# Projections with their operand differences made in place, the first branch's sum kept on chip, and blocks read from PSUM

## The chip, the cores and the metric

The kernel runs on one NeuronCore of a Trainium2 chip. The metric is the device time of one execution in microseconds. Three runs of the kernel before took 1317.86, 1319.45 and 1319.67 us; the median is 1319.45.

## The reference

One step of a hybrid encoder layer on 1024 prompt rows and 64 sample rows, D_MODEL 1024, float32. Cut to what matters here:

```
h = RMSNorm(x) * (1 + scale) + shift
z = h @ w_in                       # split into a, g_a, u, v_b, g_b, q, k, v_c, g_c, z_lr, g_m
y_a = pool_mixer(a) * silu(g_a)    # 512 columns
y_b = sgu_mixer(u, v_b) * silu(g_b)  # 512 columns
y_c = rmsnorm(gla_scan(q, k, v_c, decay)) * silu(g_c)   # 1024 columns
gm = sigmoid(g_m)                  # three parts of 1024
m = gm[0] * (y_a @ w_oa) + gm[1] * (y_b @ w_ob) + gm[2] * (y_c @ w_oc)
x = x + gate * RMSNorm_post(m @ w_out)
```

## The kernel before

Every large product is done in float32 accuracy with split operands: a "hi" part (rounded to fp32r by ScalarE, a CAST) and a "lo" part (the rest, a subtraction on VectorE or GpSimd). A step is then three matmuls, hi x hi, hi x lo and lo x hi, each once per 272-column half of a 544-column piece: six matmuls per 128 rows of depth. The 1088 tokens are two pieces p of 544 columns (512 prompt and 32 sample).

Most products are in Strassen-Winograd form. `s_unit` (line 578) makes 256 output channels from four blocks A(i, j) of a weight matrix and seven operands named in `PRODUCTS` (B11, T2, B21, T3, T1, T4, B22). `strassen_b` (line 433) makes these seven from four blocks of the input: B11, B21 and B22 as they are, and the differences T1 = b12 - b11, T2 = b22 - T1, T3 = b22 - b12, T4 = b21 - T2; each of the seven is split into hi and lo. It is called for the layer's input h (`dst is Hb`), for the first branch (`Ab`, from z_ya, two blocks j) and for the third (`Cb`, from z_yc, four blocks j). The second branch (`plain_units`, line 1443) is a plain product with operands split by `pairs_in`; its result is multiplied by its gate, added to the first branch's sum, which is loaded from `z_m` in DRAM, and stored there again.

In a unit, seven products of nkk steps go through three PSUM pairs: pA, pB and `third` (pC). B11 goes to pA, is copied by ScalarE into pB, on which T2 adds; T1 goes to pC; B21 adds onto pA, which then holds block (0, 0); T3 adds onto pB. The last two products, T4 and B22, are left over (`unfinished`) and done by `finish_unit` inside the next unit, between its B11 and the copy into pB, or at the end of a stage. T4 gives block (1, 0) in pB; the blocks (0, 1) and (1, 1) are sums that VectorE makes in the staging tiles `u` and `c22`. Every block is first copied to a staging tile by ScalarE and handed to `post(i, p, t)`: for a silu gate (`post_gc`, `post_ga`, `post_gb`) tanh on ScalarE and (th + 1) * t on VectorE, for a sigmoid gate (`post_gm`) tanh, for a branch (`post_m`) (th + 1) * t with th loaded from `z_gm`.

With `feed`, as in the first units of a projection, the first three products are interleaved step by step: each of B11, T2, T1 for block j before the next j.

Order of the work: the q, k, v, gate and mixer units of `w_in` (34 units) with the attention heads woven in, the last twelve of them gate units g_m; then `blocks_in(z_ya)` and the first branch (w_oa, four units, nkk = 2) with `pairs_in(z_yb)` woven in; the second (w_ob, 16 pieces) with `blocks_in(z_yc)` for j = 0 to 2 woven in; the third (w_oc, four units, nkk = 4), whose first unit feeds j = 3; then the output product with w_out. From the first unit on, a planner sets the order on each engine: it places instructions by priority in program order on a simulated timeline; weights are raised by `ahead()`. On the chip each engine works through its own queue in that order.

Tiles: operands lie in 56 places h (and five more, `NH` on), listed for reuse in `free` and `rest` in the order of `PRODUCTS`, since that is the order in which the last unit of the stage before lets them go; loaded blocks and gates go through a ring of 12 tiles x (`cur["blk"]`); results and differences through a ring of 9 staging tiles (`stage`, tag s). In the trace, `h` is an operand place, `T` a difference, `raw`, `sf`, `hi`, `lo` the weights' parts, `sps` pA and pB, and `t`, `c`, `u` staging tiles. All instructions stand under the line of a helper (L70, `InOrder`), so rows are told apart by tiles.

Of the kernel before, what the change touches and what calls it, by code (L numbers as in the profile page):

```python
# [24 lines left out]
PC = TH + SH  # L25
# [21 lines left out]
PLAIN = ("B11", "B21")  # L47
PRODUCTS = ("B11", "T2", "B21", "T3", "T1", "T4", "B22")
H_PLACES = (
# [29 lines left out]
def tile_hybrid_pool_sgu_gla_step(  # L79
# [353 lines left out]
    def strassen_b(dst, j, b1, b2, alloc):  # L433
        b11, b12 = b1
        b21, b22 = b2

        def put(name, src, he, le):
            hl = (alloc(name), alloc(name))
            split(src, hl, he, le)
            dst[name][j] = hl  # L440
            places[name] += alloc.held[-2:]

        t1, t2, t3, t4 = (stage("T", F32)[:, 0:PC] for _ in range(4))
        put("B11", b11, act, dve)
        dve.tensor_sub(t1, b12, b11)
        dve.tensor_sub(t2, b22, t1)
        put("T2", t2, act, dve)
        put("T1", t1, act, dve if dst is Hb and j == 3 else pool)
        with behind() if dst is Hb and j == 3 else ExitStack():
            put("B21", b21, act, dve)  # L450
            pool.tensor_sub(t3, b22, b12)
            put("T3", t3, act, dve)
            pool.tensor_sub(t4, b21, t2)
            put("T4", t4, act, dve)
            put("B22", b22, act, pool)
# [122 lines left out]
    def s_unit(src, c0, Bb, nkk, post, off=0, raw=None, feed=None):  # L578
# [64 lines left out]
        else:  # L643
# [8 lines left out]
            act.copy(view(c22), vC)  # L652
            yield nkk
        product(pA, A(0, 1), "B21", False)
        c11 = stage("c11", F32)
        act.copy(view(c11), vA)
        post(0, 0, c11)
        yield nkk
# [6 lines left out]
        def rest():  # L665
            product(pB, A(1, 1), "T4", False)
            c21 = stage("c21", F32)
            act.copy(view(c21), vB)
            post(1, 0, c21)
            yield nkk  # L670
# [208 lines left out]
    def silu2(t):  # L879
# [3 lines left out]
        dve.scalar_tensor_tensor(t, th, 1.0, t, op0=ALU.add, op1=ALU.mult)  # L883

    def post_gc(head):
        def post(i, p, t):
            silu2(t[:, 0:PC])
            store(z_gc[2 * head + i], p, t[:, 0:PC])

        return post  # L890

    def post_gm(b0):
        def post(i, p, t):
            act.activation(t[:, 0:PC], t[:, 0:PC], AF.Tanh, scale=0.5)
            store(z_gm[b0 + i], p, t[:, 0:PC])

        return post

# [71 lines left out]
    def post_ga(unit):  # L970
        def post(i, p, t):
            g = 2 * unit + i
            silu2(t[:, 0:PC])
            yp = st.pop(("yp", g, p))
            pool.tensor_mul(t[:, 0:PC], t[:, 0:PC], yp[:, 0:PC])
            store(z_ya[g], p, t[:, 0:PC])

        return post

# [96 lines left out]
    def post_gb(unit):  # L1076
        def post(i, p, t):
            g = 2 * unit + i
            t = t[:, 0:PC]
            silu2(t)  # L1080
            u = st.pop(("u", g, p))
            dve.scalar_tensor_tensor(t, t, 0.5, u[:, 0:PC], op0=ALU.mult, op1=ALU.mult)
            store(z_ub[g], p, t)

        return post

# [279 lines left out]
    def pair_in(z, p, alloc, raw_alloc):  # L1366
# [3 lines left out]
        turn[0] += 1  # L1370
        split(t, hl, act, pool if turn[0] % 3 == 0 else dve)
        return hl
# [10 lines left out]
    def w_unit(src, c0, nk, alloc=None):  # L1383

        out = []
        for k0 in range(0, nk, 4):
# [4 lines left out]
            for j in range(2):  # L1391
# [7 lines left out]
                with ahead():  # L1399
                    act.copy(hi, s)  # L1400
                    (pool if turn[0] % 2 == 0 else dve).tensor_sub(lo, s, hi.bitcast(F32))
                out += [(hi[:, i, :], lo[:, i, :]) for i in range(2)]
        return out

    def post_m(br, u):

        def fetch(i, p):
            j = 2 * u + i
            th = load(z_gm[br * 8 + j], p * PC, PC, "gm", blk)[:, 0:PC]
            return th, br and load(z_m[j], p * PC, PC, "m", blk)[:, 0:PC]  # L1410

        early = {}
        if br == 2 and u == 3:
# [4 lines left out]
        def post(i, p, t):  # L1418
            j, t = 2 * u + i, t[:, 0:PC]
            th, m = early.get((i, p)) or fetch(i, p)  # L1420
            dve.scalar_tensor_tensor(t, th, 1.0, t, op0=ALU.add, op1=ALU.mult)
            if br:
                (pool if br == 2 and (p or u < 3) else dve).tensor_add(t, t, m)
            store(z_m[j], p, t)
# [8 lines left out]

    Bp = {}

    def pairs_in(z, dst, places_):
# [6 lines left out]
    def plain_units(w, src):  # L1443

        n = 0
        for u in range(4):
            with ahead():
                wk = w_unit(w, u * UC, 4)
            for i in range(2):
                j = 2 * u + i  # L1450
                for p in range(2):
# [16 lines left out]
                    )  # L1468
                    m = load(z_m[j], p * PC, PC, "m", blk)[:, 0:PC]
                    pool.tensor_add(t, t, m)  # L1470
                    store(z_m[j], p, t)
# [306 lines left out]
    with first:  # L1778
# [106 lines left out]
        weave(last_units(), last_heads(), R3)  # L1885
        run(gate_steps, finish_unit())
        tick(LATER)
# [19 lines left out]
    def units(w, blocks, nkk, br, us=range(4)):  # L1907
        for u in us:
            yield from s_unit(
                w, u * UC, blocks, nkk, post_m(br, u), feed=None if u else fed  # L1910
            )

    cur["more"] = ctx.enter_context(tc.tile_pool(name="more", bufs=1))
    rest = [*free[28:56], *range(NH, NH + 5)]
    weave(
        chain(units(woa, Ab, 2, 0), finish_unit()),
        pairs_in(z_yb, Bp, rest[0:16]),
        0.2,
    )
    rest = [*rest[16:], *a_free]  # L1920
    weave(
        plain_units(wob, Bp),
        blocks_in(z_yc, Cb, ((j, rest[14 * j : 14 * j + 14]) for j in range(3))),
        0.08,
    )
    last = blocks_in(z_yc, Cb, ((3, rest[42:45] + free[28:39]),))
    idle = free[39:44]
    msum.append(slot(idle.pop())[:, 0:512].rearrange("p (k n) -> p k n", k=KB))
# [92 lines left out]
```

## Time and profile before

| | |
|---|---|
| median of three runs | 1319.45 us |
| the profiled execution's own time | 1318.15 us |
| its span, first to last instruction | 1316.4 us |
| mean granted TensorE clock | 0.973 |
| TensorE busy | 1217.9 us, 93% of the span |
| VectorE busy | 914.5 us, 69% |
| ScalarE busy | 626.2 us, 48% |
| GpSimd busy | 444.2 us, 34% |
| DMA | 195.38 MB, mean 148 GB/s |

The span of the trace begins at 0 us. The last gate unit's products end near 984 us, the first branch's near 1040, the second's near 1092, the third's near 1189, and the output product follows. A matmul in the trace overlaps its neighbours, so a stretch in which TensorE is busy all the time can still hold more or fewer matmuls; the count per microsecond is the better measure.

### The profile page before, as it was taken

The numbers are of one execution on the slowest core, as the hardware profiler recorded it, in microseconds if no ns is written. First come the engines' busy times: TensorE is split into PE (matmuls) and PEld (weight loads), VectorE is DVE, ScalarE is ACT, GpSimd is POOL, SyncE is SP. The second block draws the span as 40 slices with busy tenths as digits, with TensorE's granted clock in tenths as the row PEclk, the third lists the DMA queues.
The fourth block names the chain that finished last, engine by engine and source line by source line (L and its number), as shares of the span: only waits on it lengthen the run. The fifth ranks groups of instructions, "written<-read, shape, count | busy, mean of one in ns | idle before, by whom it ended". The sixth has DMA issues, their size and how long they took to land.

```text
span 1316.4 us, 23815 instructions
## 1 busy us (share of the span) xinstructions
PE 1217.9 (93%) x8962; PEld 1139.5 (87%) x8962; DVE 914.5 (69%) x1507; ACT 626.2 (48%) x1259; POOL 444.2 (34%) x356
## 2 busy tenths in 40 slices
PE   5779999999999999999999999999997998996895
PEld 3279999998999999999999999999896997994674
DVE  6976845557746679675476969665467798669758
ACT  7547734454553434544444464544364423343533
POOL 4640211122411315131145322212132486448524
PEclk9889999999999999999999999999999999998898
DMA  8612533252332213323146444445446898665055
GB/s 285 200 50 99 179 107 93 75 162 90 120 102 80 84 57 100 120 72 119 33 138 219 152 159 146 156 124 157 134 137 213 301 333 294 210 231 185 23 198 201
DMA packets 144609, 195.38 MB, mean 148 GB/s; under 512 B 18505, under 2 KB 82047, under 8 KB 144494
## 3 DMA queue, kind: packets, MB, share of 16 engines
q1 hardware_dynamic: 144494, 193.86, 45.3%
q8 instruction: 70, 1.15, 0.4%
q14 instruction: 45, 0.37, 0.1%
HBM read 133.59 MB, written 60.22 MB: 147 GB/s over the span
## 4 chain that ended last, share of the span: by engine, by line
PE 62%; DVE 13%; DMA 10%; issue 8%; POOL 3%; ACT 2%; SPq 1%; DVEq 0%; POOLq 0%; ACTq 0%
PE sps L70 37%; PE third L70 15%; PE aps L70 9%; DVE x L70 4%; DVE h L70 3%; DVE lo L70 1%; DMA x<-z_bc 1%; DMA raw<-in_w_in_dram 1%; DMA h<-z_m 1%; DMA x<-z_yc 1%; DMA h<-in_x_prompt_dram 1%; SPq L72 1%; DMA h<-in_ada_w_dram 1%; POOL T L70 1%; DMA x<-z_yb 1%
## 5 line engine op out<-in xcount | busy, mean ns | idle before, releaser
L70 PE MATMUL sps<-h,hi 128*128 128x272 f32 x3344 | 588.4, 295 | 14.9 <-DVE h L70 4.5
L70 PEld LDWEIGHTS sps<-h,hi 128*128 128x128 f32 x3344 | 482.6, 190 | 24.7 <-DVE h L70 4.9
L70 PE MATMUL sps<-h,lo 128*128 128x272 f32 x1672 | 353.5, 291 | 0.0
L70 PEld LDWEIGHTS sps<-h,lo 128*128 128x128 f32 x1672 | 265.8, 190 | 2.3 <-issue 1.7
L70 PE MATMUL third<-h,hi 128*128 128x272 f32 x1344 | 237.5, 294 | 6.8 <-ACT h L70 1.9
L70 PEld LDWEIGHTS third<-h,hi 128*128 128x128 f32 x1344 | 193.9, 189 | 11.7 <-issue 3.1
L70 DVE TENSOR_TENSOR lo<-sf,hi 128x512 fp32r<-128x512 f32 (+1 forms) x168 | 119.5, 712 | 92.7 <-ACT hi L70 87.3
L70 ACT CAST hi<-sf 128x512 fp32r<-128x512 f32 (+1 forms) x168 | 100.2, 598 | 157.7 <-PE sps L70 119.2
L70 POOL TENSOR_TENSOR sf<-raw 128x512 f32<-128x512 f32 (+1 forms) x38 | 49.5, 1301 | 303.7 <-DVE lo L70 238.4
L70 DVE TENSOR_TENSOR lo<-raw,hi 128x512 fp32r<-128x512 f32 (+1 forms) x130 | 99.2, 764 | 73.8 <-ACT hi L70 54.6
L70 ACT CAST hi<-raw 128x512 fp32r<-128x512 f32 (+1 forms) x134 | 80.1, 599 | 144.4 <-PE sps L70 97.2
L70 PE MATMUL third<-h,lo 128*128 128x272 f32 x672 | 142.4, 291 | 1.2 <-DVE lo L70 1.1
L70 POOL TENSOR_TENSOR x<-x,x 128x256 f32<-128x256 f32 (+2 forms) x71 | 74.9, 1065 | 123.3 <-ACT x L70 89.2
L70 PEld LDWEIGHTS third<-h,lo 128*128 128x128 f32 x672 | 106.8, 190 | 1.7 <-DVE lo L70 1.6
L70 POOL TENSOR_TENSOR sf<-raw,sf 128x512 f32<-128x512 f32 (+1 forms) x38 | 49.3, 1298 | 170.6 <-DVE lo L70 165.7
L70 ACT ACTIVATE x<-x 128x512 f32<-128x512 f32 (+2 forms) x104 | 57.5, 568 | 89.8 <-DVE x L70 80.2
L70 DVE TENSOR_TENSOR x<-x 128x256 f32<-128x256 f32 (+4 forms) x142 | 76.6, 571 | 27.8 <-DMA x<-z_bc 16.7
L70 DVE TENSOR_TENSOR x<-x,x 128x256 f32<-128x256 f32 (+4 forms) x100 | 64.2, 656 | 9.2 <-ACT x L70 8.8
L70 DVE TENSOR_TENSOR h<-h,h 128x544 fp32r<-128x544 f32 (+4 forms) x47 | 53.2, 1150 | 11.9 <-DMA h<-in_w_out_dram 6.9
L70 PE MATMUL aps<-x,x 128*128 128x256 f32 (+6 forms) x352 | 54.4, 290 | 2.3 <-ACT vt L70 1.8
L70 DVE TENSOR_TENSOR sf<-raw,raw 128x512 f32<-128x512 f32 (+1 forms) x42 | 33.0, 785 | 30.2 <-POOL sf L70 29.9
L70 POOL TENSOR_TENSOR sm<-sm,nhalf 128x1 f32<-128x1 f32 (+3 forms) x36 | 26.8, 748 | 75.4 <-DVE sm L70 75.4
(273 smaller groups left out, 1797.1 us busy)
## 6 DMA issues: line engine op xcount, KB each, us to landing
raw<-in_w_in_dram SPq DMA_DIRECT2D x68, 512.0 KB, 3.8
x<-z_gm SPq DMA_DIRECT2D x48, 272.0 KB, 3.3
z_gm<-c SPq DMA_DIRECT2D x36, 272.0 KB, 2.3
x<-z_m SPq DMA_DIRECT2D x32, 272.0 KB, 4.5
h<-z_m SPq DMA_DIRECT2D x28, 272.0 KB, 5.1
h<-in_x_prompt_dram SPq DMA_DIRECT2D x28, 256.0 KB, 5.4
z_m<-c SPq DMA_DIRECT2D x24, 272.0 KB, 2.4
h<-in_ada_w_dram SPq DMA_DIRECT2D x24, 256.0 KB, 4.5
```

The lines of the kernel that those rows point to most:

```text
L70: return f(*args, **kw)
L72: self._last = f(*args, **kw)
```

## The change

- `strassen_b` for the branches (not for Hb): one staging tile t2 in place of four; T1 is written over b11, T3 over b12, T4 over b21. The order is B11, T2, T1, B21, T3, T4, B22, and so is `PRODUCTS`. The low parts of T1 and B22 go from GpSimd to VectorE, as do the second branch's (a third of them) and half of w_ob's; T3's and T4's differences stay on GpSimd.
- `s_unit`: the blocks (0, 0) and (1, 0) go through `out`: where the post has a `direct` form, it works from PSUM, without the copy.
- The first branch's products by its gate are written to 16 places `m_first` on chip and not stored; the second branch adds them with VectorE, where it loaded `z_m` and added with GpSimd.
- The first branch's first unit has no `feed`; the last gate unit's T4 and B22 are left over into it.
- The places: operands of the second branch on the last places of the unit before and four more; the third branch's blocks 0 and 1 on those of the first branch, 2 on two further places and on `m_first`'s, 3 on the rest and on the second branch's. One place more in all.

```
@@ -45,7 +45,7 @@
 PLAIN = ("B11", "B21")
-PRODUCTS = ("B11", "T2", "B21", "T3", "T1", "T4", "B22")
+PRODUCTS = ("B11", "T2", "T1", "B21", "T3", "T4", "B22")
 H_PLACES = (
...
@@ -440,13 +440,28 @@
+        if dst is not Hb:
+            t2 = stage("T", F32)[:, 0:PC]
+            put("B11", b11, act, dve)
+            dve.tensor_sub(b11, b12, b11)
+            dve.tensor_sub(t2, b22, b11)
+            put("T2", t2, act, dve)
+            put("T1", b11, act, dve)
+            put("B21", b21, act, dve)
+            pool.tensor_sub(b12, b22, b12)
+            put("T3", b12, act, dve)
+            pool.tensor_sub(b21, b21, t2)
+            put("T4", b21, act, dve)
+            put("B22", b22, act, dve)
+            return
+
         t1, t2, t3, t4 = (stage("T", F32)[:, 0:PC] for _ in range(4))
...
         put("T2", t2, act, dve)
-        put("T1", t1, act, dve if dst is Hb and j == 3 else pool)
-        with behind() if dst is Hb and j == 3 else ExitStack():
+        put("T1", t1, act, dve if j == 3 else pool)
+        with behind() if j == 3 else ExitStack():
             put("B21", b21, act, dve)
...
@@ -651,10 +666,17 @@
             yield nkk
+        def out(i, ps):
+            direct = getattr(post, "direct", None)
+            if direct:
+                direct(i, 0, ps)
+            else:
+                t = stage("c", F32)
+                act.copy(view(t), ps)
+                post(i, 0, t)
+
         product(pA, A(0, 1), "B21", False)
-        c11 = stage("c11", F32)
-        act.copy(view(c11), vA)
-        post(0, 0, c11)
+        out(0, vA)
         yield nkk
...
@@ -664,9 +686,7 @@
             product(pB, A(1, 1), "T4", False)
-            c21 = stage("c21", F32)
-            act.copy(view(c21), vB)
-            post(1, 0, c21)
+            out(1, vB)
             yield nkk
...
@@ -882,18 +902,37 @@
+    def silu2_of(ps):
+
+        th, t = blk("th")[:, 0:PC], stage("t", F32)[:, 0:PC]
+        act.activation(halves(th), ps, AF.Tanh, scale=0.5)
+        dve.scalar_tensor_tensor(halves(t), halves(th), 1.0, ps, op0=ALU.add, op1=ALU.mult)
+        return t
+
+    def silu_post(done):
+
+        def post(i, p, t):
+            t = t[:, 0:PC]
+            silu2(t)
+            done(i, p, t)
+
+        post.direct = lambda i, p, ps: done(i, p, silu2_of(ps))
+        return post
+
     def post_gc(head):
-        def post(i, p, t):
-            silu2(t[:, 0:PC])
-            store(z_gc[2 * head + i], p, t[:, 0:PC])
-
-        return post
+        return silu_post(lambda i, p, t: store(z_gc[2 * head + i], p, t))
...
+        def direct(i, p, ps):
+            t = stage("t", F32)[:, 0:PC]
+            act.activation(halves(t), ps, AF.Tanh, scale=0.5)
+            store(z_gm[b0 + i], p, t)
+
+        post.direct = direct
         return post
...
@@ -968,14 +1007,13 @@
     def post_ga(unit):
-        def post(i, p, t):
+        def done(i, p, t):
             g = 2 * unit + i
-            silu2(t[:, 0:PC])
             yp = st.pop(("yp", g, p))
-            pool.tensor_mul(t[:, 0:PC], t[:, 0:PC], yp[:, 0:PC])
-            store(z_ya[g], p, t[:, 0:PC])
-
-        return post
+            pool.tensor_mul(t, t, yp[:, 0:PC])
+            store(z_ya[g], p, t)
+
+        return silu_post(done)
...
@@ -1074,15 +1112,13 @@
     def post_gb(unit):
-        def post(i, p, t):
+        def done(i, p, t):
             g = 2 * unit + i
-            t = t[:, 0:PC]
-            silu2(t)
             u = st.pop(("u", g, p))
...
-        return post
+        return silu_post(done)
...
@@ -1368,7 +1404,7 @@
         turn[0] += 1
-        split(t, hl, act, pool if turn[0] % 3 == 0 else dve)
+        split(t, hl, act, dve)
         return hl
...
@@ -1398,7 +1434,7 @@
                     act.copy(hi, s)
-                    (pool if turn[0] % 2 == 0 else dve).tensor_sub(lo, s, hi.bitcast(F32))
+                    dve.tensor_sub(lo, s, hi.bitcast(F32))
                 out += [(hi[:, i, :], lo[:, i, :]) for i in range(2)]
...
@@ -1408,6 +1444,13 @@
             return th, br and load(z_m[j], p * PC, PC, "m", blk)[:, 0:PC]
+
+        def place(i, p):
+
+            if br:
+                return stage("t", F32)[:, 0:PC]
+            t = m_first[2 * u + i, p] = slot(m_places[4 * u + len(m_first) % 4])
+            return t
...
@@ -1416,11 +1459,27 @@
         def post(i, p, t):
-            j, t = 2 * u + i, t[:, 0:PC]
             th, m = early.get((i, p)) or fetch(i, p)
-            dve.scalar_tensor_tensor(t, th, 1.0, t, op0=ALU.add, op1=ALU.mult)
-            if br:
-                (pool if br == 2 and (p or u < 3) else dve).tensor_add(t, t, m)
+            src = t[:, 0:PC]
+            t = src if br else place(i, p)
+            dve.scalar_tensor_tensor(t, th, 1.0, src, op0=ALU.add, op1=ALU.mult)
+            done(i, p, t, m)
+
+        def direct(i, p, ps):
+            th, m = early.get((i, p)) or fetch(i, p)
+            t = place(i, p)
+            dve.scalar_tensor_tensor(
+                halves(t), halves(th), 1.0, ps, op0=ALU.add, op1=ALU.mult
+            )
+            done(i, p, t, m)
+
+        post.direct = direct
+
+        def done(i, p, t, m):
+            j = 2 * u + i
+            if not br:
+                return
+            (pool if p or u < 3 else dve).tensor_add(t, t, m)
             store(z_m[j], p, t)
...
@@ -1432,6 +1491,7 @@
     Bp = {}
+    m_first, m_places = {}, []
...
@@ -1466,8 +1526,7 @@
                     )
-                    m = load(z_m[j], p * PC, PC, "m", blk)[:, 0:PC]
-                    pool.tensor_add(t, t, m)
+                    dve.tensor_add(t, t, m_first.pop((j, p)))
                     store(z_m[j], p, t)
...
@@ -1883,7 +1942,7 @@
         weave(last_units(), last_heads(), R3)
-        run(gate_steps, finish_unit())
+        run(gate_steps)
         tick(LATER)
...
@@ -1907,24 +1966,27 @@
             yield from s_unit(
-                w, u * UC, blocks, nkk, post_m(br, u), feed=None if u else fed
+                w, u * UC, blocks, nkk, post_m(br, u), feed=None if u or not br else fed
             )
...
     cur["more"] = ctx.enter_context(tc.tile_pool(name="more", bufs=1))
-    rest = [*free[28:56], *range(NH, NH + 5)]
+    m_places.extend(free[28:44])
+    b_places = [*free[44:56], *range(NH, NH + 4)]
     weave(
         chain(units(woa, Ab, 2, 0), finish_unit()),
-        pairs_in(z_yb, Bp, rest[0:16]),
+        pairs_in(z_yb, Bp, b_places),
         0.2,
     )
-    rest = [*rest[16:], *a_free]
+    c_places = [*a_free, NH + 4, NH + 5, *m_places]
+    for p in range(2):
+        c_places += [i for n, i in enumerate(b_places) if n // 2 % 2 == p]
     weave(
         plain_units(wob, Bp),
-        blocks_in(z_yc, Cb, ((j, rest[14 * j : 14 * j + 14]) for j in range(3))),
+        blocks_in(z_yc, Cb, ((j, c_places[14 * j : 14 * j + 14]) for j in range(3))),
         0.08,
     )
-    last = blocks_in(z_yc, Cb, ((3, rest[42:45] + free[28:39]),))
-    idle = free[39:44]
+    last = blocks_in(z_yc, Cb, ((3, c_places[42:56]),))
+    idle = c_places[56:]
     msum.append(slot(idle.pop())[:, 0:512].rearrange("p (k n) -> p k n", k=KB))
...
```

## Rows read from the trace of the kernel before

**Rows 1.** The page's busy times: busy us (share of the span) xinstructions.

```profile
PE 1217.9 (93%) x8962; PEld 1139.5 (87%) x8962; DVE 914.5 (69%) x1507; ACT 626.2 (48%) x1259; POOL 444.2 (34%) x356
```

**Rows 2.** Windows: stretch, us, busy us (xcount) of PE to POOL, clock, DMA share, GB/s.

```profile
984.00:1002.00 18.00, 10.50 (x63) 9.39 (x62) 18.00 (x23) 11.01 (x22) 9.45 (x6) 0.81 0.59 191
1002.00:1040.00 38.00, 34.52 (x265) 33.25 (x263) 26.13 (x48) 18.38 (x40) 5.45 (x6) 1.00 0.83 278
1040.00:1092.00 52.00, 49.20 (x386) 48.48 (x386) 46.82 (x41) 15.93 (x28) 45.77 (x28) 1.00 0.94 324
1092.00:1115.00 23.00, 16.56 (x108) 15.06 (x107) 21.13 (x21) 10.66 (x19) 14.94 (x9) 0.93 0.78 284
1115.00:1181.00 66.00, 65.60 (x523) 65.37 (x522) 41.28 (x57) 25.84 (x45) 27.87 (x26) 1.00 0.67 215
```

**Rows 3.** Timeline of TensorE, 984 to 996: start, us, instruction [idle before, releaser].

```profile
985.87 0.39 PE L70 MATMUL sps<-h,hi 128*128 128x272 f32 x1 [0.46 <-ACT h L70]
990.55 1.05 PE L70 MATMUL sps<-h,hi 128*128 128x272 f32 x3 [4.30 <-DVE h L70]
```

**Rows 4.** Timeline of VectorE, 981 to 996.

```profile
986.84 1.89 DVE L70 TENSOR_TENSOR T<-x,T 128x544 f32<-128x544 f32 x1
988.64 1.86 DVE L70 TENSOR_TENSOR h<-T,h 128x544 fp32r<-128x544 f32 x1
```

**Rows 5.** Timeline of TensorE, 1092 to 1115.

```profile
1099.83 0.77 PE L70 MATMUL sps<-h,hi 128*128 128x272 f32 x4 [1.76 <-DVE t L70]
...
1106.21 0.95 PE L70 MATMUL third<-h,hi 128*128 128x272 f32 x3 [1.03 <-POOL h L70]
```

**Rows 6.** Groups of VectorE, 984 to 1115: busy us, mean ns | idle before.

```profile
L70 DVE TENSOR_TENSOR h<-T,h 128x544 fp32r<-128x544 f32 x18 | 21.6, 1214 | 3.3 <-ACT h L70 2.8
L70 DVE TENSOR_TENSOR h<-x,h 128x544 fp32r<-128x544 f32 x12 | 13.1, 1115 | 3.2 <-ACT h L70 3.2
...
L70 DVE SCALAR_TENSOR_TENSOR t<-x,sps 128x544 f32<-128x544 f32 x11 | 7.6, 707 | 0.0
...
L70 DVE TENSOR_TENSOR sf<-raw,raw 128x256 f32<-128x256 f32 x2 | 0.8, 414 | 0.0
```

**Rows 7.** Groups of GpSimd, 984 to 1115.

```profile
L70 POOL TENSOR_TENSOR t<-t,x 128x544 f32<-128x544 f32 x16 | 26.9, 1698 | 7.1 <-DVE t L70 4.5 <-issue 2.7
...
L70 POOL TENSOR_TENSOR h<-T,h 128x544 fp32r<-128x544 f32 x6 | 10.0, 1664 | 3.2 <-ACT h L70 3.2
...
L70 POOL TENSOR_TENSOR h<-x,h 128x544 fp32r<-128x544 f32 x5 | 7.8, 1551 | 11.5 <-ACT h L70 11.5
L70 POOL TENSOR_TENSOR lo<-raw,hi 128x512 fp32r<-128x512 f32 x4 | 6.8, 1700 | 0.2 <-ACT hi L70 0.2
```

**Rows 8.** Windows, VectorE alone: stretch, us, busy us (xcount), clock, DMA.

```profile
959.00:984.00 25.00, 14.16 (x20) 1.00 0.45 144
```

**Rows 9.** Tile z_m: time of its transfers.

```profile
DMA to landing us min/median/max: 2.0/4.7/7.1
```

**Rows 10.** Timeline of ScalarE in a silu gate unit, 341.5 to 345.2.

```profile
342.01 0.60 ACT L70 COPY c<-sps 128x544 f32<-128x544 f32 x1
342.65 0.66 ACT L70 ACTIVATE th<-c 128x544 f32<-128x544 f32 x1
343.21 0.61 ACT L70 COPY sps<-sps 128x544 f32<-128x544 f32 x1
```

**Rows 11.** Timeline of TensorE in the same unit: the ends of T4 and B22.

```profile
341.29 0.41 PE L70 MATMUL sps<-h,lo 128*128 128x272 f32 x2
...
345.06 0.67 PE L70 MATMUL sps<-h,hi 128*128 128x272 f32 x4
```

**Rows 12.** Tile c: xcount, ns min/median/max, first and last start.

```profile
L70 DVE SCALAR_TENSOR_TENSOR c<-th,c x12: 711/724/1435, 214.7 to 405.3; 128x544 f32<-128x544 f32 x12
```

**Rows 13.** Waits of TensorE, 100 to 957: us in total, times, longest.

```profile
PE sps L70 <- ACT sps L70: 1.1, 2, 0.6
```

**Rows 14.** Windows of 33 us over the attention heads.

```profile
825.00:858.00 33.00, 31.07 (x247) 30.20 (x246) 21.42 (x40) 18.39 (x40) 10.23 (x11) 0.95 0.43 144
```

## The prediction

> **What bounds the kernel now.** I read the busy times of the page first. TensorE is busy 93% of the span [rows 1], so time can come only from its idle or slow stretches, or from fewer matmuls; the change issues the same matmuls. The table by stage comes next. The units of w_oc at their steady pace, from 1115, run 523 matmuls in 66.00 us, 0.126 us apiece [rows 2]; that pitch is the yardstick. Against it the reader sees four stretches around the three branch projections:
>
> - 984 to 1002, start of the first branch: 63 matmuls are 7.9 us of work in 18 us, 10.1 lost, at a granted clock of 0.81;
> - 1002 to 1040, rest of the first branch: 265 matmuls, 33.4 of 38 us, 4.6 lost;
> - 1040 to 1092, second branch: 386, 48.6 of 52, 3.4 lost;
> - 1092 to 1115, start of the third branch: 108, 13.6 of 23, 9.4 lost.
>
> Together 27.5 us of 131 are lost. VectorE is busy 18.0 + 26.1 + 46.8 + 21.1 = 112 of these 131 us, GpSimd 75.6 [rows 2]. The timelines then say who was late. From 986.25 TensorE stands 4.30 us until VectorE has made an operand tile h, and goes on at 990.55 [rows 3]. VectorE at that moment works through differences T and their low parts in single file, two of them at 1.89 and 1.86 us [rows 4]. At 1099.83 it stands 1.76 us for VectorE's evacuation t, at 1106.21 for a low part made by GpSimd [rows 5]. So these stretches are bound by the operand builder, VectorE above all, and not by TensorE.
>
> Why is VectorE slow there? The table of its operations from 984 to 1115 [rows 6] has 128x544 low parts from SBUF at means of 1214 and 1115 ns, while the product that reads PSUM (t<-x,sps) takes 707 ns. In the timeline the 1.8 us pieces lie where GpSimd works too. Counting each of the 21 groups of that view at its best time (about 0.71 us for 544 columns, 0.69 for 512, 0.41 for 256), some 37 us of VectorE's time are such stretching. GpSimd's own rows for those 131 us [rows 7]: the 16 additions of the second branch 26.9 us, low parts 10.0 + 7.8 + 6.8.
>
> **The change part by part**, against the profiled execution's 1318.15 us (span 1316.4, 1.75 around it), which is 0.1% under the median of 1319.45.
>
> *1. The first branch's first unit loses its interleaved form, and the last gate unit's two left-over products now run inside it.* Before, those two products ended at about 984 with nothing behind them but three products interleaved by block, which need T2 and T1 of both blocks at once. Now B11 (12 matmuls, 1.5 us) needs only plain splits, then come the two left-over products (48 matmuls, 6.0 us), and only then T2. In the same stretch strassen_b writes differences into the loaded blocks and takes one staging tile, not four, so its subtractions need not wait for the nine-slot ring in which the gate units' results wait for their stores. VectorE is busy 14.16 of the 25 us before 984 [rows 8]; 10.8 us are free for a build of 18 operations (2 blocks, 2 differences and 7 low parts each) at 0.71, 12.8 us, several of which are done there already. I take 3 of the 10.1 us as still lost: gain 7. Bounds: a gain of 3 (VectorE keeps its order and only the 6.0 us of cover count, half of it used up by the reordering) and of 10.
>
> *2. Low parts leave GpSimd.* Of the two operand builds 12 (T1 and B22 in six blocks), 4 of w_ob and about 3 of the second branch's operands: 19 x 0.71 = 13.5 us more on VectorE.
>
> *3. The first branch's sum stays on chip.* 16 stores and 16 loads of 272 KB (4.5 MB each way) go; a z_m transfer takes a median 4.7 us to land [rows 9]. DMA share in 1040 to 1092 is 0.94 [rows 2], so these were not free, and the x ring of 12 slots gets 16 fewer tenants, so z_yc can be fetched sooner. The 16 additions go from GpSimd (1698 ns each [rows 7]) to VectorE: 16 x 0.71 = 11.4 us.
>
> *4. What 2 and 3 do to VectorE in the 131 us.* 13.5 + 11.4 = 24.9 us added; about ten operations of part 1 leave to before 984, 7 us; GpSimd loses 26.9 + 10.0 + 7.8 + 6.8 = 51.5 of 75.6 us, 68%, and with it I count 68% of the 37 us of stretching, 25 us. Net 112 - 7 = 105 us, beside 822 matmuls, 103 us. The two are level, and neither can be packed fully. VectorE idled 19 us in the stretch before; I take 14 (its new work is independent additions that fill holes). That gives 119 us, 12 less than 131. By stretch: 7 at the start; nothing between 1002 and 1040, where the second branch's splits arrive, since their places are the gate unit's last operands and come free only at about 984 (bounds: 3 gained, 4 lost); nothing in 1040 to 1092, where the third branch's first block, which had free places before and could start early, must wait for the first branch's (3 gained, 5 lost); 5 at the start of the third branch, where the four blocks meet less GpSimd (0 to 9 gained).
>
> *5. Blocks read from PSUM.* Two of a unit's four blocks take the direct form where their post has one: 24 blocks of the sigmoid gates, 16 of the silu gates, 16 of the first and third branch. Each saves a ScalarE copy of 0.60 us [rows 10], which is off the path: TensorE is full there. The wait that this adds: the second half tile must be free before ScalarE copies the first partial sum into it, ahead of T2. In a silu unit before, T4 ends at 341.70, copy, tanh and copy end at 343.82, and T2 starts at 345.06 [rows 10, 11], 1.24 us later. Now tanh 0.66, VectorE's product 0.72 [rows 12] and the copy 0.61 follow each other: 0.31 + 1.99 + a few hand-overs, about 2.5 us, so about 0.9 us of cover remain. Behind that copy on ScalarE wait the weights' high parts, and for those TensorE. The sigmoid gates lose 0.6 us from the same chain. I take 0; bounds: 1 gained (the whole wait for that copy between 100 and 957 is 1.1 us [rows 13]), 4 lost. The direct form of the first and third branch needs its gate tile from z_gm while it holds PSUM; no product waits on that load now, 0.
>
> [...]
>
> Sum: 1318.15 - 7 - 5 = 1306.15; **1306 us**. All lost time regained and 1 more: 1290. All bad bounds: 3 gained, 4 + 5 + 4 lost: 1328.
>
> **The rivals.**
>
> *VectorE becomes the bound and little is won.* For: it has 105 us of work against TensorE's 103, and it now does the additions on which the release of staging tiles depends. If it idles as much as before (19 us), the stretch takes 124 to 126 us: 1312. Against: its idle was mostly in 1002 to 1040, which the moved low parts fill.
>
> *The silu units stop TensorE (slower).* Eight units (four gc, two ga, two gb) have the chain tanh, VectorE, copy before T2. VectorE is fed by the attention heads there. If its product comes over 0.9 us late, TensorE stands, and short stands are followed by a lower granted clock: the 33 us from 825, with 1.93 us of idle, have it at 0.95 [rows 14], which is 1.65 us lost besides. At 2.0 + 1.65 us a unit, 29 us: 1306 + 29 = 1335. It decides against the kernel from 1.5 us a unit. Against: the planner has the heads' matmuls to put in between.
>
> *Full cover.* The build ends before 984, z_yc is early, and half of the rest is regained: 27.5 - 7 = 20.5 gained, 1298.
>
> *Nothing.* The start's wait is only put off, as VectorE's queue keeps its order, and the third branch waits as before: within 2.6 us of 1319.
>
> **How the numbers follow.** Forecast 0.48 (1301 to 1310), little won 0.20, silu units 0.12, full cover 0.14, nothing 0.06. Range: 1294 to 1317 leaves out the slower case, most of "nothing" and the deep end of "full cover", about 0.2. What 0.2% means here is 2.6 us, about what a measurement can tell. Faster: 0.48 + 0.18 + 0.14 = 0.80; same: 0.06 + 0.02 = 0.08; slower 0.12.
>
> **What would show it.** Part 1: no idle over 2 us on TensorE between the last gate unit and the second unit of the first branch, and a granted clock near 1.00 there. Parts 2 to 4: VectorE's 544-column low parts near 0.75 us; GpSimd at some 24 us in the three branches; no additions t<-t,x on GpSimd; the stretch from the gates' end to the third branch's steady pace at about 119 us. Part 5: T2 of the silu units without idle before it. Wrong, if the stretch before 984 is longer by more than 2 us, or if VectorE is above 115 us in the three branches.

## The result: 1298.28 us, and the profile after

The changed kernel takes 1298.28 us (median of four runs, 1296.94 to 1302.87), against 1319.56 for the kernel before in the same comparison: a ratio of 0.9842, 95% interval 0.9814 to 0.987. The forecast was 1306 us in a range of 1294 to 1317; the result lies in that range, but not in the 1301 to 1310 that I called the forecast proper. The profiled execution took 1297.43 us with a span of 1295.6.

The page's busy times of the changed kernel, where [rows 1] had those before: TensorE's is 9 us shorter for the same matmuls, ScalarE has 56 instructions fewer, GpSimd 55 us less.

```profile
PE 1208.5 (93%) x8962; PEld 1132.6 (87%) x8962; DVE 903.5 (70%) x1541; ACT 593.8 (46%) x1203; POOL 389.1 (30%) x321
```

To compare kernels whose stages lie at other times, I cut all traces at the same matmuls: the 60th, 123rd, 388th, 774th and 882nd of the last 1440 that have 272 columns. In the kernel before these cuts are at 984.2, 1002.5, 1041.5, 1092.9 and 1116.3, next to the stretches of [rows 2]. The windows of the changed kernel between the cuts, columns as in [rows 2]:

```profile
985.30:996.10 10.80, 8.43 (x65) 8.24 (x66) 9.00 (x18) 5.65 (x12) 0.73 (x1) 1.00 0.94 304
996.10:1033.10 37.00, 34.44 (x267) 33.48 (x267) 27.20 (x51) 18.06 (x39) 5.71 (x6) 1.00 0.60 182
1033.10:1083.40 50.30, 48.70 (x389) 48.51 (x388) 48.81 (x69) 16.13 (x27) 8.17 (x5) 1.00 0.87 286
1083.40:1098.30 14.90, 13.79 (x111) 13.58 (x110) 14.63 (x20) 6.94 (x12) 4.81 (x3) 1.00 0.74 237
```

To be read from them: the granted clock is 1.00 in all four, where it was 0.81 and 0.93 in the first and last; GpSimd has 8.2 and 4.8 us in the last two, where it had 45.8 and 14.9; VectorE is now busy 99.6 of 113.0 us. The stretch of the three branches shrank from 132.1 to 113.0 us:

| us | start of first | rest of first | second | start of third | sum |
|---|---|---|---|---|---|
| before | 18.3 | 39.0 | 51.4 | 23.4 | 132.1 |
| changed | 10.8 | 37.0 | 50.3 | 14.9 | 113.0 |
| forecast gain | 7 | 0 | 0 | 5 | 12 |
| measured gain | 7.5 | 2.0 | 1.1 | 8.5 | 19.1 |

The rest of the 20.7 us between the two profiled executions: 1.8 gained before the 500th matmul (at 141 us; up to there every engine has the same instructions in the same order before and after, and over all kernels below this point lies between 140.4 and 144.2), 2.9 lost from there to the branches, 0.4 and 2.3 gained in the third branch's steady part and in the output product.

At the start of the first branch, where TensorE had stood 4.30 us for VectorE [rows 3], its timeline now has two short waits:

```profile
986.41 0.74 PE L70 MATMUL third<-h,hi 128*128 128x272 f32 x4 [1.14 <-DVE u L70]
...
989.42 0.77 PE L70 MATMUL sps<-h,hi 128*128 128x272 f32 x4 [1.26 <-ACT sps L70]
```

VectorE makes the first difference (now x<-x,x, in place) at 958, inside the last gate unit. Its timeline there, where [rows 4] had the differences after 984:

```profile
958.05 0.72 DVE L70 TENSOR_TENSOR x<-x,x 128x544 f32<-128x544 f32 x1
...
973.21 1.34 DVE L70 TENSOR_TENSOR h<-x,h 128x544 fp32r<-128x544 f32 x2
```

The second of these rows also shows that two operations of 0.71 us each end 1.34 us after the first began: operations that follow one another without idle start about 0.63 us apart.

VectorE's groups in the three branches, to be read against [rows 6]: the low parts fell from means of 1214 and 1115 ns to 760, and the additions that came from GpSimd take 792.

```profile
L70 DVE TENSOR_TENSOR h<-x,h 128x544 fp32r<-128x544 f32 x31 | 23.2, 760 | 2.6 <-ACT h L70 2.6
L70 DVE TENSOR_TENSOR t<-t,h 128x544 f32<-128x544 f32 x16 | 12.6, 792 | 0.1
...
L70 DVE SCALAR_TENSOR_TENSOR t<-x,sps 128x544 f32<-128x544 f32 x12 | 8.6, 713 | 0.8 <-PE sps L70 0.8
```

And GpSimd's, against [rows 7]: the differences T4 (x<-x,T) and T3 (x<-x,x) are the largest that is left.

```profile
L70 POOL TENSOR_TENSOR x<-x,T 128x544 f32<-128x544 f32 x4 | 6.9, 1714 | 38.1 <-ACT h L70 14.1 <-issue 12.1 <-DVE T L70 11.8
L70 POOL TENSOR_TENSOR x<-x,x 128x544 f32<-128x544 f32 x4 | 6.4, 1606 | 16.9 <-DVE x L70 7.7 <-DMA x<-z_gm 5.5 <-PE sps L70 3.7
```

### The profile page after: what moved, and what is told of

It reads as the page before. It is cut to its first block, busy times and chain, and to the rows that moved or that the text cites. A ratio compares the mean times of both kernels' runs of the same rounds, so it can differ in the third digit from the quotient of the medians.

```text
span 1295.6 us, 23667 instructions
## 1 busy us (share of the span) xinstructions
PE 1208.5 (93%) x8962; PEld 1132.6 (87%) x8962; DVE 903.5 (70%) x1541; ACT 593.8 (46%) x1203; POOL 389.1 (30%) x321
## 5 line engine op out<-in xcount | busy, mean ns | idle before, releaser
L70 PE MATMUL third<-h,hi 128*128 128x272 f32 x1344 | 234.3, 292 | 2.1 <-DVE u L70 2.0
L70 DVE TENSOR_TENSOR lo<-raw,hi 128x512 fp32r<-128x512 f32 (+1 forms) x134 | 95.9, 718 | 69.3 <-ACT hi L70 55.9
L70 POOL TENSOR_TENSOR sf<-raw 128x512 f32<-128x512 f32 (+1 forms) x38 | 49.9, 1313 | 306.5 <-DVE lo L70 265.2
L70 POOL TENSOR_TENSOR x<-x,x 128x256 f32<-128x256 f32 (+3 forms) x77 | 82.0, 1073 | 166.2 <-ACT x L70 90.3
L70 POOL TENSOR_TENSOR sf<-raw,sf 128x512 f32<-128x512 f32 (+1 forms) x38 | 49.9, 1314 | 153.5 <-DVE lo L70 149.9
L70 DVE TENSOR_TENSOR x<-x 128x256 f32<-128x256 f32 (+4 forms) x142 | 73.8, 552 | 29.3 <-DMA x<-z_bc 16.5
L70 DVE TENSOR_TENSOR x<-x,x 128x256 f32<-128x256 f32 (+5 forms) x105 | 65.4, 636 | 9.2 <-ACT x L70 8.5
L70 ACT CAST h<-x 128x544 fp32r<-128x544 f32 (+1 forms) x62 | 38.5, 642 | 33.4 <-DMA x<-z_yc 9.4
L70 DVE TENSOR_TENSOR h<-x,h 128x544 fp32r<-128x544 f32 (+1 forms) x57 | 48.6, 870 | 4.1 <-ACT h L70 4.0
L70 DVE TENSOR_TENSOR sf<-raw,raw 128x512 f32<-128x512 f32 (+1 forms) x42 | 29.0, 691 | 32.1 <-POOL sf L70 31.8
```

Source lines behind the costliest of these rows:

```text
L70: return f(*args, **kw)
```

## The experiments

Ratios are to the kernel before, measured beside each; the stages, cut as above, are those of one profiled execution each.

| kernel | median us | ratio, 95% interval | start of first, rest, second, start of third | sum |
|---|---|---|---|---|
| changed | 1298.28 | 0.9842, 0.9814 to 0.987 | 10.8, 37.0, 50.3, 14.9 | 113.0 |
| e1 | 1297.85 | 0.9853, 0.9832 to 0.9875 | 13.5, 33.9, 49.2, 18.7 | 115.3 |
| e2 | 1313.42 | 0.9967, 0.995 to 0.9985 | 15.2, 36.7, 57.7, 15.3 | 124.9 |
| e3 | 1302.08 | 0.9886, 0.9871 to 0.9901 | 10.8, 36.6, 49.9, 18.8 | 116.1 |
| e4 | 1304.87 | 0.9895, 0.9874 to 0.9916 | 11.5, 38.5, 50.2, 15.1 | 115.3 |
| e5 | 1309.36 | 0.9943, 0.9916 to 0.9969 | 16.9, 36.8, 48.5, 19.9 | 122.1 |
| e6 | 1299.03 | 0.9863, 0.9835 to 0.9891 | 10.8, 35.8, 48.4, 19.2 | 114.2 |
| e7 | 1310.73 | 0.993, 0.9903 to 0.9957 | 10.9, 36.9, 52.8, 23.2 | 123.8 |
| e8 | 1293.53 | 0.9822, 0.9805 to 0.9839 | 10.8, 36.6, 50.2, 15.2 | 112.8 |
| e9 | 1311.49 | 0.9959, 0.9942 to 0.9975 | 16.3, 35.7, 52.8, 21.8 | 126.6 |
| e11 | 1294.95 | 0.9819, 0.9785 to 0.9853 | 10.8, 34.4, 49.2, 20.2 | 114.6 |
| e12 | 1294.12 | 0.9802, 0.9777 to 0.9827 | 9.1, 36.7, 48.6, 15.6 | 110.0 |

**e7: the differences in place, alone, on the kernel before.**

```
+        if dst is not Hb:
+            t2 = stage("T", F32)[:, 0:PC]
...
+            dve.tensor_sub(b11, b12, b11)
...
+            put("T1", b11, act, pool)
...
+            pool.tensor_sub(b12, b22, b12)
...
+            pool.tensor_sub(b21, b21, t2)
...
+            put("B22", b22, act, pool)
+            return
```

> The kernel before with one part of the change: the branches' differences written over the loaded blocks, with one staging tile, in the new order; T1's and B22's low parts stay on GpSimd and nothing else moves. Theory (the staging ring held the first branch's build back, as four tiles in the changed kernel cost 11 us): the first difference is made at about 960 us, the start of the first branch (18.3 us before) is 3 to 6 us shorter, total 1310 to 1316. Rival (early differences are worth something only with the places and VectorE's low parts): start within 2 us of 18.3, total 1316 to 1320.

The theory held, and the start gained more than its 3 to 6 us. VectorE's timeline has the first difference in the last gate unit, and the start of the branch is 10.9 us, 7.4 less than before and as short as in the changed kernel:

```profile
957.09 0.72 DVE L70 TENSOR_TENSOR x<-x,x 128x544 f32<-128x544 f32 x1
```

**e5: the changed kernel with four staging tiles for the differences.**

```
-            t2 = stage("T", F32)[:, 0:PC]
+            t1, t2, t3, t4 = (stage("T", F32)[:, 0:PC] for _ in range(4))
...
-            dve.tensor_sub(b11, b12, b11)
+            dve.tensor_sub(t1, b12, b11)
...
```

> The changed kernel with four staging tiles for the differences, not written over the loaded blocks; engines and order as changed. Theory (the staging ring held the differences back): the first difference of the first branch is made after 975 us, where the changed kernel has it at 958, and the start of the first branch loses 3 to 7 us; at the third branch's start 0 to 3 more; total 1301 to 1307. Rival (the order of the operands and the engines decide, the ring does not): the difference is made at about 958 again and the total is 1297 to 1300.

The theory's direction held: the start of the first branch loses 6.1 us. The third's loses 5.0, more than its 0 to 3, the total lies above its band, and VectorE's first difference comes at 971.8, not after 975. The order of the operands is the changed kernel's here, so the order alone does not bring the early build of e7 (VectorE's timeline, then TensorE's):

```profile
971.81 0.72 DVE L70 TENSOR_TENSOR T<-x,x 128x544 f32<-128x544 f32 x1
```

```profile
987.21 1.27 PE L70 MATMUL sps<-h,hi 128*128 128x272 f32 x4 [4.52 <-ACT sps L70]
```

**e4: the interleaved first unit and the early end of the gate units, in the changed kernel.**

```
-        run(gate_steps)
+        run(gate_steps, finish_unit())
...
-                w, u * UC, blocks, nkk, post_m(br, u), feed=None if u or not br else fed
+                w, u * UC, blocks, nkk, post_m(br, u), feed=None if u else fed
```

> The changed kernel, but the first branch's first unit has its interleaved form again and the last gate unit's two products end before it. Theory (the build of the first branch's operands is done before 984 us because the differences need no staging tiles, so the cover of 6 us is not what counts): TensorE loses 0 to 3 us at the start of the first branch, total 1298 to 1301. Rival (the cover is what counts, as part 1 of the forecast had it): 5 to 7 us of the 7.5 won there are lost, total 1303 to 1306, with an idle of over 3 us on VectorE's h at the start.

At the start it costs 0.7 us, as the theory said, so the cover is not what was won there. No wait of TensorE in that stretch is over 0.8 us; the longest two:

```profile
PE third L70 <- DVE lo L70: 0.8, 1, 0.8
PE third L70 <- ACT c L70: 0.8, 1, 0.8
```

The median is nevertheless 6.6 us above the changed kernel's, in the rival's band and more than the 2.3 us of the branches. The profiled execution took 1300.22, the fastest of four, so what the others lost isn't in a trace; whether they lost it at the start stays open.

**e2: the low parts on GpSimd again, in the changed kernel.**

```
-            put("T1", b11, act, dve)
+            put("T1", b11, act, pool)
...
-            put("B22", b22, act, dve)
+            put("B22", b22, act, pool)
...
-        split(t, hl, act, dve)
+        split(t, hl, act, pool if turn[0] % 3 == 0 else dve)
...
-                    dve.tensor_sub(lo, s, hi.bitcast(F32))
+                    (pool if turn[0] % 2 == 0 else dve).tensor_sub(lo, s, hi.bitcast(F32))
```

> The changed kernel with the low parts that moved (T1 and B22 of the branches' operands, a third of the second branch's operands, half of w_ob) on GpSimd again; the second branch's additions stay on VectorE. Theory (GpSimd beside VectorE stretches VectorE's low parts): VectorE's 128x544 low parts go from a mean of 0.76 us to 0.9 or more, the second branch and the start of the third (65 us in the changed kernel) take 3 to 8 us more, total 1301 to 1306. Rival (VectorE only changes what it is busy with, 19 operations less for it is relief): those stretches stay or get shorter, 1298 or less.

The theory held for the low parts (965 ns) and for the two stretches (7.8 us more); the loss of 15 us in all was larger than it said, 11.9 of it in the branches. VectorE has 19 operations less to do, and yet in the branches it is busy 102.0 us, against 99.6 in the changed kernel. These are its low parts and GpSimd's there, and TensorE's two longest waits.

```profile
L70 DVE TENSOR_TENSOR h<-x,h 128x544 fp32r<-128x544 f32 x20 | 19.2, 965 | 3.9 <-ACT h L70 3.8
...
L70 DVE TENSOR_TENSOR lo<-raw,hi 128x512 fp32r<-128x512 f32 x8 | 9.6, 1216 | 0.0
```

```profile
L70 POOL TENSOR_TENSOR h<-x,h 128x544 fp32r<-128x544 f32 x10 | 16.3, 1634 | 16.8 <-ACT h L70 8.6 <-DVE t L70 8.2
```

```profile
PE third L70 <- DVE u L70: 4.5, 1, 4.5
PE third L70 <- DVE t L70: 3.9, 1, 3.9
```

Before each of the two, VectorE works without a pause through low parts that are stretched, 1.88 and 1.54 us from 989.42, 3.63 for two from 1077.23, and only then makes the u or t that TensorE waits for. Over the branches as a whole most of the lost time is idle time of VectorE, 22.9 us against 13.4.

**e3: the second branch's additions on GpSimd.**

```
-                    dve.tensor_add(t, t, m_first.pop((j, p)))
+                    pool.tensor_add(t, t, m_first.pop((j, p)))
```

> The changed kernel with the second branch's 16 additions on GpSimd again (the first sum still on chip). Theory (GpSimd's work stretches VectorE's, as for the low parts): VectorE loses 11 us of additions but its 128x544 low parts go to 0.9 us or more beside 27 us of GpSimd; second branch and start of the third together 0 to 5 us longer than 65 us; total 1298 to 1303. Rival (VectorE is the bound and gets 16 operations less): those two stretches are 3 to 8 us shorter, total 1290 to 1295.

The theory's figures were met: the two stretches take 68.7 us against 65.2, the total is 1302.08, and the low parts are stretched again:

```profile
L70 DVE TENSOR_TENSOR h<-x,h 128x544 fp32r<-128x544 f32 x31 | 27.5, 903 | 7.1 <-ACT h L70 5.9 <-POOL t L70 1.3
```

But VectorE, with 16 operations less, is busy 96.3 us in the branches, 3.3 less than in the changed kernel, and idle 19.8, 6.4 more. What lengthens the branches is thus not VectorE's load; whether it is single stretched operations at the wrong moment or the 1.7 us that an addition takes on GpSimd, this run does not separate.

**e6: the first sum through DRAM.**

```
             if not br:
+                store(z_m[j], p, t)
                 return
...
-                    dve.tensor_add(t, t, m_first.pop((j, p)))
+                    m = load(z_m[j], p * PC, PC, "m", blk)[:, 0:PC]
+                    m_first.pop((j, p))
+                    dve.tensor_add(t, t, m)
```

> The changed kernel, but the first branch's products are also stored to z_m, and the second branch adds what it loads from there, as before (16 stores and 16 loads of 272 KB, with their places in the ring x); the addition stays on VectorE. Theory (those transfers were hidden, VectorE was the bound): 0 to 3 us more, total 1298 to 1301. Rival (the transfers held up the third branch's blocks at a DMA share of 0.94): second branch and start of the third are 5 us or more longer than 65 us, total 1303 to 1308, and ScalarE waits for z_yc as it did before.

The theory held: the total is the same within the intervals. The third branch's start is 4.3 us longer, but the second branch is 1.9 and the stretches before it 1.2 us shorter; the 32 transfers are nearly hidden, 1.2 us in the branches.

**e9: VectorE's additional work alone, on the kernel before.**

```
-        put("T1", t1, act, dve if dst is Hb and j == 3 else pool)
+        put("T1", t1, act, dve if dst is not Hb or j == 3 else pool)
...
-            put("B22", b22, act, pool)
+            put("B22", b22, act, pool if dst is Hb else dve)
...
-        split(t, hl, act, pool if turn[0] % 3 == 0 else dve)
+        split(t, hl, act, dve)
...
-                    (pool if turn[0] % 2 == 0 else dve).tensor_sub(lo, s, hi.bitcast(F32))
+                    dve.tensor_sub(lo, s, hi.bitcast(F32))
...
-                    pool.tensor_add(t, t, m)
+                    dve.tensor_add(t, t, m)
```

> The kernel before, with only the engines changed: the branches' low parts of T1 and B22, the second branch's low parts, w_ob's, and the second branch's additions are all on VectorE. No places, order or forms are changed. Theory (taking GpSimd away from VectorE's side is most of the gain, and low parts alone were worth 15 us in e2): 8 to 14 us faster than before, 1305 to 1311. Rival (it is the places and the on-chip sum that make it pay; without them VectorE is only loaded more): within 4 us of before, 1314 or above.

Between the two: 0.41% faster, about 5.4 us, and 5.5 us of the branches. Neither band was met. The move pays by itself, but under a third of what taking it away costs in the changed kernel (15.1 and 3.8 us in e2 and e3).

**e1: all blocks through the copy.**

```
-            direct = getattr(post, "direct", None)
+            direct = None
```

> The changed kernel, but every block (0, 0) and (1, 0) is copied to a staging tile by ScalarE again, as before. Theory (VectorE's relief and the early build carry the gain, reading from PSUM carries none): 0 to 3 us slower than the changed kernel, so 1298 to 1301 us, and the three branches stay at 112 to 115 us. Rival (the missing copies carry a third or more of the gain, since ScalarE also makes the high parts): 7 us or more lost, 1305 us or above, with ScalarE's waits in the branches longer.

The theory held to within half a microsecond: the total is the changed kernel's, so reading from PSUM brought nothing in sum. But its parts moved. The branches are 2.3 us longer, and the stretch before them shorter. From the 1500th to the 3500th matmul of 272 columns, where the silu units lie, e1 takes 323.5 us and the changed kernel 328.3 (before: 323.6).

**e8: the silu gates alone through the copy.**

```
-        post.direct = lambda i, p, ps: done(i, p, silu2_of(ps))
```

> The changed kernel, but the silu gates' blocks go through the copy again; the sigmoid gates and the first and third branch read PSUM. In the copies everywhere (e1) the stretch from 195 to 660 us, where the silu units lie, has 3.9 us of idle on TensorE, in the changed kernel 9.2. Theory (the silu units' chain tanh, VectorE, copy before T2 stops TensorE, the rest of the direct forms is neutral or helps a little): that idle falls to about 4 us, the branches stay at 113 us, total 1290 to 1294. Rival (the difference between the two is the planner's chance, not the silu chain): idle of 7 us or more and a total of 1296 to 1300.

The theory held: 1293.53 us, though its interval and the changed kernel's overlap, so the totals alone do not part the two. The waits of TensorE from 195 to 660 us, the changed kernel first:

```profile
PE sps L70 <- DVE c L70: 2.1, 3, 1.1
...
PE sps L70 <- ACT sps L70: 1.4, 2, 0.8
PE third L70 <- DVE u L70: 0.9, 1, 0.9
```

and e8, where the last two of these kinds are gone and 4.2 us of waits are left of 9.4, those for the attention heads (aps) for the most part:

```profile
PE aps L70 <- ACT vt L70: 1.8, 3, 1.3
PE aps L70 <- DVE x L70: 1.4, 1, 1.4
PE aps L70 <- ACT x L70: 0.7, 1, 0.7
PE sps L70 <- DVE c L70: 0.3, 1, 0.3
```

Over all thirteen kernels, one trace each, the 1500th to the 3500th of these matmuls take 325.9 to 330.2 us in the six that read the silu gates' blocks from PSUM (mean 328.3), and 322.2 to 326.1 in the seven that copy (mean 323.9): 4.4 us. So the price of the silu units' direct form is shown. The chain itself in the one unit where its copy ends a wait of TensorE, ScalarE, then VectorE, then TensorE of the changed kernel, against [rows 10, 11]:

```profile
342.95 0.61 ACT L70 ACTIVATE th<-sps 128x544 f32<-128x544 f32 x1
344.44 0.60 ACT L70 COPY sps<-sps 128x544 f32<-128x544 f32 x1 [0.87 <-DVE t L70]
```

```profile
343.69 0.71 DVE L70 SCALAR_TENSOR_TENSOR t<-th,sps 128x544 f32<-128x544 f32 x1
```

```profile
345.09 0.77 PE L70 MATMUL sps<-h,hi 128*128 128x272 f32 x4 [0.79 <-ACT sps L70]
```

**e11: the first branch through the copy too.**

```
-        post.direct = direct
+        if br:
+            post.direct = direct
```

> e8 (silu gates by the copy) and also the first branch by the copy; the sigmoid gates and the third branch read PSUM. In e8 TensorE stands 0.75 to 1.26 us before T2 in each of the first branch's four units, 3.7 us in all, for a ScalarE copy that waits behind VectorE's product from PSUM; with copies everywhere (e1) these waits are not there. Theory (the products are only 1.5 us long there, so the chain over VectorE is too long for them): these four waits go, total 1289 to 1292, 1 to 4 us under e8's 1293.5. Rival (ScalarE's two copies a unit take the place, and the start of the branch gets longer as in e1, 13.5 against 10.8 us): 1293 to 1296.

The total is in the rival's band, level with e8. The waits before T2 in the first branch went, as the theory said, but for the 1.26 us at its start (rest of the first 34.4 us against 36.6), and the start is not longer, against the rival; but the third's start gave it back, 20.2 against 15.2. That VectorE, busy 98.8 of the 114.6 us, only pays at the next stage what one stage gains, is my reading and not shown.

**e12: the differences on VectorE too, with e8's copies.**

```
-            pool.tensor_sub(b12, b22, b12)
+            dve.tensor_sub(b12, b22, b12)
...
-            pool.tensor_sub(b21, b21, t2)
+            dve.tensor_sub(b21, b21, t2)
```

> e8 with the differences T3 and T4 of the branches' operands on VectorE too, so that GpSimd does almost nothing in the three branches. Theory (an operation of GpSimd costs VectorE about what it would take itself): VectorE's 544-column low parts fall from 0.76 to 0.72 us, total within 2 us of e8, 1291 to 1295. Rival (VectorE is the bound, 12 operations of 0.71 us are 8.5 us of delay): 1297 to 1302.

The theory held: 1294.12 us, branches 2.8 us shorter than e8's, low parts at 720 ns.

```profile
L70 DVE TENSOR_TENSOR h<-x,h 128x544 fp32r<-128x544 f32 x31 | 21.8, 720 | 3.6 <-ACT h L70 3.5
```

With 0.9802 (0.9777 to 0.9827) it has the lowest ratio of all to the kernel before; the intervals do not part it from e8 or from the changed kernel.

## Why the prediction was right, and where its terms were not

*The place and the mechanism* were right in the main: the gain is in the three branches, and it comes from work taken off GpSimd (e2, e3, e9) and from an earlier build of the operands (e7, e5). That the first of these works by VectorE's stretched operations alone is not shown: it fits e2's two long waits, but in e2 and e3 most of the lost time is idle time of VectorE.

*The total* is 7.7 us under the forecast. It is the number of the rival "full cover", 1298, to which I gave 0.14. As that rival had it, TensorE waits for no operand at the start of the first branch, and the first load of z_yc starts early, at 997.7 us instead of 1007.7. In part the total is luck: 1.8, 0.4 and 2.3 us were gained where nothing was forecast and no cause was sought, and 2.9 lost.

*Part 1, a gain of 7 at the start:* 7.5 measured. Of its two reasons one carried it. The staging ring held the build back (e7 alone gives the whole 7.4 us); the cover of 6 us by the left-over products, which the text put first, is worth 0.7 us there (e4).

*Part 4, 119 us for the stretch:* 113.0, the term that was mis-sized. I forecast VectorE's busy time to fall by 7, from 112 to 105; at the same cuts it fell from 113.2 to 99.6. The count of operations rose by 24, from 131 to 155, and at best times by 16.7 us (forecast 17.9); the stretching fell from 37.2 to 10.4 us (26.8; forecast 25). These two make up 3 of the 6.6 us that VectorE was spared beyond the forecast. The other 3.5 are a step that failed: I added durations, but operations that follow one another start 0.63 us apart and not 0.71, so the summed durations exceed the busy time by 10.8 us now and by 7.3 before, and the added ones cost less than I charged. VectorE's idle time, 14 us in the forecast, is 13.4. By stage, about half of the 7.1 us that the branches gained beyond the forecast came at the third's start, 8.5 for 5.

*Part 3:* the transfers of z_m, which I called not free at a DMA share of 0.94, are nearly hidden: 1.2 us in the branches (e6).

*Part 5, taken as 0:* its sum is 0 (e1), but by luck: 4.4 us are lost in the silu units, and the direct forms elsewhere give about as much back (e8 is 4.3 us under e1, with intervals that overlap). The rival of the silu units foresaw the place of the loss; its price was far too high, as TensorE stands 0.3 to 1.1 us at a time and not 2, and the granted clock of 195 to 660 us is 1.00 as before. Its mechanism, a product of VectorE that comes late, is not what the unit above shows: VectorE starts 0.12 us after the tanh ends. ScalarE comes late, with the tanh 2.2 us after T4's last matmul (340.77 to 342.95) where I had reckoned 0.31, because until 343.04 it is at another tile's and a weight's operations. Only 0.79 us of waiting ends with such a chain's copy; of the rest most ends with VectorE's c and u, and how the direct form brings those about is open. I had said that the forecast would be wrong if the stretch before 984 grew by more than 2 us; it ends 1.1 us later, but the 2.9 us lost there are hidden by the 1.8 gained before it. VectorE's products t<-x,sps, read from PSUM, took a mean of 713 ns in the branches, against 711 at best from SBUF [rows 12].

*"VectorE becomes the bound and little is won":* VectorE is busy 99.6 of the 113.0 us, nearly all of the stretch, and yet 19 us were won.

*The output product's 2.3 us* were not forecast. Kernels with the places of before need 126.9 to 128.4 us from the last branch matmul to the end, those with the new places 124.9 to 126.2, but e5 127.5; nothing was tried on it, and it stays open.

## What to carry to other kernels

Before an operation is given to GpSimd, charge it with what it costs VectorE beside it. Here 1.7 us of GpSimd made a single two-input operation of VectorE on SBUF up to 1.2 us longer (1.91 against 0.71 at best, in the kernel before). As an estimate, from VectorE's summed durations in the branches less the same operations at their best times, each operation that went from one engine to the other in e2, e3, e9 and e12 changed VectorE's stretching by 0.4 to 0.8 us on average: about the 0.7 us for which VectorE does the work itself, so that the move to GpSimd relieved VectorE of little or nothing. Temporary tiles from a ring that results also use held back a build by 14 us (e5); writing over an operand that is no longer needed frees it. Without the copy out of PSUM, whatever stands in its place comes before the next use of the half tile. In the silu unit shown under e8 the last read ended 3.6 us after T4's last matmul, 2.2 of them until ScalarE began; in the kernel before, the copy had ended 0.9 us after it [rows 10, 11]. In the silu units, where two engines in turn read PSUM, the direct form cost 4.4 us (the means under e8); in the first branch, where one does, it cost nothing in the total (e8 without the copy 1293.53 us, e11 with it 1294.95).

## What the runs showed of the hardware

In the branches VectorE's products t<-x,sps, which read PSUM, kept means of 707 to 715 ns in all thirteen kernels, with GpSimd busy 7 to 76 us beside them, while low parts of the same width from SBUF ranged from 0.71 to 1.91 us. TensorE's granted clock, at 0.81 and 0.93 in the first and last stretch of the branches before, was 1.00 in both after the change, where no wait is over 1.3 us. At the start of the first branch it is low again where a long wait is back: 0.80 with one of 4.52 us (e5), 0.78 with 4.54 (e2), 0.87 with 3.82 (e1). After the 4.52 us of e5 the next 22 matmuls took 5.14 us, 2.4 more than at the 0.126 apiece of the steady pace; after the 4.30 us of the kernel before [rows 3] the next 16 took 3.51, 1.5 more. These two waits cost more than their length.
